# Hybrid recurrent/MoE decoder block: routing order, 8 KB weight runs, the order of the last expert pair and final norm, and the engines of the recurrence split

## The chip, the core and the metric

The kernel runs on one core of one Trainium2 chip. The metric is device time in microseconds (us) for one call; the changed kernel and the kernel before are timed in the same way. The core's engines are named as in the profile: PE (TensorE, matmuls), PEld (its weight loads), DVE (VectorE), ACT (ScalarE), POOL (GpSimd) and SP (the queue that issues the loads). The data are float32 throughout.

## What is computed

One decoder block over 512 tokens and 16 meta tokens, width 1024. Two mixers run side by side on the normed input (HGRN2, a gated linear recurrence of four heads, and RG-LRU, a convolution with a gated scan), are merged by two gates and projected. A mixture of experts follows: every token takes one of 4 groups and in it 2 of 8 experts, so that 32 experts of 3 x 2 MB of weights (gate, up, down) are all read once, 201 MB in all. Cut to the lines that matter here:

```python
def mixer(hn, w_in, ...):
    proj = hn @ w_in
    q_pre, f_pre, i_pre, og_pre, lx, ly, ga, gb = jnp.split(proj, idx, axis=-1)
    o_a = hgrn2_branch(q_pre, f_pre, i_pre, og_pre, lb, hg_norm_g)
    o_b = rglru_branch(lx, ly, conv_w, conv_b, w_r, b_r, w_i, b_i, lam)   # ends: h * gelu(ly)
    return (sigmoid(ga) * (o_a @ w_up_a) + sigmoid(gb) * (o_b @ w_up_b)) @ w_out

h = h + mixer(rmsnorm(h, norm1_g), ...)
hf = rmsnorm(h, norm2_g)
# group_logits -> top-1 group; exp_logits inside it -> top-2 experts and their weights
y = (silu(xb @ w_gate[e]) * (xb @ w_up[e])) @ w_down[e]      # xb: the tokens of expert e
h = h + sum over the two experts of weight * y
return rmsnorm(h, final_g)[:, N_META:]
```

## The kernel before, in words

**Mixers.** All products of the first half are made float32-exact from two fp32r parts: `split` (line 86) writes the rounded high part of a tensor with one engine and the rest (low part, a subtraction) with another. Weights come from `raw` slots and are split into three `hl` slots by `hl_tile`, high part by ACT or DVE (L88, L90), low part by POOL (L91); the matmuls of `dense` (L205) use high and low of both sides. The RG-LRU (`lru`, L623) walks over pairs of blocks; `finish` (L696) makes the scan of a pair, multiplies it by the gelu branch (`ge`, L711) and splits the result into `obH` and `obL` (L712), eight times in all. `merge` (L805) then needs the weights of the gates first, and `obH`/`obL` only for the product with `w_up_b`. PE and DVE and ACT are ordered by a scheduler in this half.

**Routing.** From line 1074 on, PE and DVE run in the order in which the code is written (`manual_schedule`). For each tile t of 128 tokens: `last` (output projection), `early` (square sum, transposes to `hT`, L900), `logits` (L922), `choose` (L928, then a row of small DVE operations that ends in `SEL`), `slots0` (rank of each token in its experts, L942, and the one-hot matrix `OH0` of the first expert pair, L978) and `dispatch` (L1105: two matmuls of 512 columns with `OH0` gather the tokens of the first pair into `px`). `XG`, its transpose `XS` and the first gate product follow.

**Experts.** The loop at L1158 takes two experts at a time (16 pairs, 64 token slots each, on the two column halves of PE). Weights come in pieces of 1 MB (L760, on SP) into some twenty slots; a piece holds two of the eight (gate, up) or one of the four (down) 128-row slices of **both** experts, so that one partition of it is two runs of 4 KB, one of each expert. A slot is free again when its last matmul has read it, and SP issues the next piece into it. PE per pair: `pgt` (gate), `pw`, `put` (up), `combine` of the pair before (`pcb`, L1055), transposes, `py` (down).

**The end.** The last pair's down weights come in half pieces (512 columns, runs of 2 KB). After the last pair each of the four token tiles gets its residual add (L1226, DVE), square sum (L1227, ACT), scaling (L1229, ACT; power on POOL, L1230), and two halves of the output: columns 0 to 511 by ACT or POOL in turn (L1233, L1235), 512 to 1023 by DVE (L1236), then the store (L1237).

Of the kernel before, what the change touches and what calls it, by code (L numbers as in the profile page):

```python
# [38 lines left out]
def hybrid_block_kernel(ctx: ExitStack, tc: tile.TileContext, x, meta, norm1_g, w_in, hg_lb,  # L39
# [583 lines left out]
    def lru():  # L623
# [6 lines left out]
        for b0 in range(0, NB, 2):  # L630
# [65 lines left out]
            def finish(b0=b0, bs=bs, XC=XC, RR=RR, TH=TH, GE=GE):  # L696
# [7 lines left out]
                for i, b in enumerate(bs):  # L704
# [7 lines left out]
                    split(obH[b // 4][:, b % 4], obL[b // 4][:, b % 4], ge, DVE, POOL)  # L712
# [28 lines left out]

    EW = [(w[0].rearrange("e (p k) c -> p e k c", p=128), nk) for w, nk in ((w_gate, 8), (w_up, 8), (w_down, 4))]
    last_p = NE // 2 - 1
    CUTS = [[(k, k + 2, 0, 512) for k in range(0, 8, 2)]] * 2 + [[(k, k + 1, 0, 1024) for k in range(4)]]
    pieces, pieces0 = [], []
    for p_ in range(last_p + 1):
        for m in range(3):
            cuts = CUTS[m]
            if p_ == 0 and m == 0:
                cuts = cuts[:2]  # L750
                pieces0 = [(0, 0, k, k + 1, 0, 512) for k in range(4, 8)]
            if p_ == last_p and m == 2:
                cuts = [(k, k + 1, c, c + 512) for c in (0, 512) for k in range(4)]
# [3 lines left out]

    def fetch(t_, s, piece):
        m, p, k0, k1, c0, c1 = piece
        SP.dma_start(t_, EW[m][0][:, 2 * p:2 * p + 2, k0:k1, c0:c1])  # L760
        for k in range(k0, k1):
            at.setdefault((m, p), {})[k, c0 // 512] = (t_[:, :, k - k0], c0, s)

    def prefetch(n=len(pieces)):
        while n and nxt[0] < len(pieces) and free:
# [3 lines left out]
            t_, s = slot([128, 2, piece[3] - piece[2], piece[5] - piece[4]], F32, "wx")  # L769
            fetch(t_, s, piece)  # L770

    def weight(tab, e, k, c0):

        t_, b, _ = tab.get((k, c0 // 512)) or tab[k, 0]
        return t_[:, e, c0 - b:c0 - b + 512]

    def take(m, p):
        tab = at.pop((m, p))
        return tab, sorted({s for _, _, s in tab.values() if s})
# [322 lines left out]
    def dispatch(t):  # L1102

        for half in range(2):
            PE.matmul(px[half], OH0[:, t], tk(h32, t, 512 * half, 512 * half + 512), start=(t == 0), stop=(t == 3))  # L1105
# [22 lines left out]
    dispatch(0)  # L1128
    early(3)
    choose(2, pls[2])  # L1130
    slots0(1)
    dispatch(1)
    pls.append(logits(3, hts[3]))
    slots0(2)
    choose(3, pls[3])
    dispatch(2)
    slots0(3)
    dispatch(3)
# [10 lines left out]
    SW = []  # L1149

    def feed(m, p, f):
        tab, ss = take(m, p)
        r = f(tab)
        give(*ss)
# [3 lines left out]
    for p in range(last_p + 1):  # L1158
# [14 lines left out]
        if p == last_p:  # L1173
            combine(back, 0)
            gfb = ms("A", [128, D], F32, "gfb")
            for half in range(2):
# [4 lines left out]
                ACT.activation(gfb[:, 512 * half:512 * half + 512], p_.rearrange("t a b -> t (a b)"), AF.Copy)  # L1181
        pu = feed(1, p, lambda w2: up_proj(w2, "put"))
# [135 lines left out]
```

## Time and profile before

| | us |
|---|---|
| median of 3 runs | 990.17 (989.74 to 991.3) |
| profiled execution, its own time | 990.63 |
| its span | 988.9 |
| PE busy | 917.6 (93%) |
| DVE / ACT / POOL busy | 453.1 / 255.9 / 247.8 |
| product lines: mixers `pj` L205 (hnH and hnL) | 251.8 and 149.1 |
| expert products `put`, `pgt`, `py` | 119.1, 115.7, 114.7 |

The span is cut into 40 slices on the page. PE reads 7 to 9 tenths in every slice, but matmuls are pipelined and their ends are modelled, so that this alone doesn't tell what bounds a stage. The transfer row tells it: 44 to 263 GB/s until slice 18, then 410, 334, 276, 373, and 408 to 410 in every slice up to the 38th. The granted clock of PE is 0.983 in the mean.

### The profile page before, as it was taken

Reading aid. Unit: us, or ns where it says so; the run is one execution under the profiler, and the core shown is the slowest. Engines: PE = TensorE matmul, PEld = TensorE weight load, DVE = VectorE, ACT = ScalarE, POOL = GpSimd, SP = SyncE. Lnnn points to the kernel's source line nnn. Section 1 sums busy time; section 2 is a strip of 40 time slices with the busy share of each in tenths; the row PEclk is TensorE's granted clock in tenths of the full one; section 3 lists DMA queues with packets and bytes.
Section 4 is the critical chain, followed back from the end, with each engine's and each line's share of the span. In section 5 each row is a group of like instructions: output and inputs, shape, how many; then the busy total and the mean of one; then the engine's idle time right before and its main releaser. Section 6 shows DMA issues by size and latency. Waiting matters only on the chain. (4 is left out here: it accounts for less than half of the span.)

```text
span 988.9 us, 12070 instructions
## 1 busy us (share of the span) xinstructions
PE 917.6 (93%) x4756; PEld 590.2 (60%) x4756; DVE 453.1 (46%) x924; ACT 255.9 (26%) x455; POOL 247.8 (25%) x167
## 2 busy tenths in 40 slices
PE   7989999989988999999978999999998988889893
PEld 5979998979967888888733444444442433323341
DVE  5668458786784323323552443343431433224323
ACT  6445535966760000000310111000010100011013
POOL 3542442344456454555100000000000000000004
PEclk9989999999999999999999999999999999999997
DMA  6222112112472322239979999999999999999982
GB/s 217 66 73 77 44 54 86 54 55 86 159 263 85 99 92 92 79 128 410 334 276 373 408 408 408 408 408 408 408 409 408 410 408 409 408 408 409 409 346 88
DMA packets 94151, 251.45 MB, mean 254 GB/s; under 512 B 6507, under 2 KB 39359, under 8 KB 94090
## 3 DMA queue, kind: packets, MB, share of 16 engines
q1 hardware_dynamic: 91352, 244.61, 64.7%
q0 software_dynamic: 2160, 3.91, 1.1%
q10 hardware_dynamic: 578, 2.10, 0.5%
q8 instruction: 39, 0.64, 0.3%
q14 instruction: 22, 0.18, 0.0%
HBM read 250.37 MB, written 4.19 MB: 257 GB/s over the span
## 5 line engine op out<-in xcount | busy, mean ns | idle before, releaser
L205 PE MATMUL pj<-hnH,hl 128*128 128x512 f32 (+1 forms) x960 | 251.8, 352 | 10.5 <-POOL hl L91 8.2
L91 POOL TENSOR_TENSOR hl<-raw,hl 128x1024 fp32r<-128x1024 f32 (+1 forms) x76 | 174.7, 2301 | 196.1 <-ACT hl L88 99.6
L205 PEld LDWEIGHTS pj<-hnH,hl 128*128 128x128 f32 x960 | 163.0, 191 | 34.4 <-POOL hl L91 9.5
L205 PE MATMUL pj<-hnL,hl 128*128 128x512 f32 (+1 forms) x480 | 149.1, 348 | 0.0
L1022 PE MATMUL put<-wx,XS 128*64 128x512 f32 x512 | 119.1, 606 | 18.6 <-DMA wx<-in_w_up_dram 18.5
L1022 PE MATMUL pgt<-wx,XS 128*64 128x512 f32 x512 | 115.7, 601 | 3.0 <-DMA wx<-in_w_gate_dram 2.7
L1041 PE MATMUL py<-wx,HG 128*64 128x512 f32 x512 | 114.7, 596 | 2.4 <-DMA wx<-in_w_down_dram 1.7
L995 POOL DMA_INDIRECT XG<-HD,idx x15 | 15.1, 1008 | 400.2 <-DVE OHT L1002 382.5
L205 PEld LDWEIGHTS pj<-hnL,hl 128*128 128x128 f32 x480 | 85.0, 191 | 10.1
L1022 PEld LDWEIGHTS put<-wx,XS 128*64 128x64 f32 x512 | 34.0, 137 | 89.6 <-issue 53.8
L1022 PEld LDWEIGHTS pgt<-wx,XS 128*64 128x64 f32 x512 | 36.5, 138 | 78.4 <-issue 69.5
L1058 DVE TENSOR_TENSOR h<-h,pcb 128x512 f32<-128x512 f32 x124 | 75.5, 679 | 7.4 <-PE pcb L1055 7.4
L1041 PEld LDWEIGHTS py<-wx,HG 128*64 128x64 f32 x512 | 34.8, 137 | 69.7 <-issue 60.6
L1028 DVE SCALAR_TENSOR_TENSOR HG<-put,sw,HG 128x512 f32<-128x512 f32 x16 | 12.0, 752 | 120.6 <-PE put L1022 114.8
L1049 DVE SCALAR_TENSOR_TENSOR Y<-py,sw,Y 128x512 fp32r<-128x512 f32 x31 | 23.3, 751 | 89.9 <-ACT Y L1048 89.9
L90 DVE CAST hl<-raw 128x1024 fp32r<-128x1024 f32 (+1 forms) x40 | 35.7, 892 | 58.4 <-PE pj L205 58.4
L1055 PE MATMUL pcb<-Y,OHT 128*128 128x512 f32 x248 | 62.0, 401 | 0.0
L1036 ACT ACTIVATE HG<-pht 128x512 f32<-128x512 f32 x16 | 9.6, 598 | 195.1 <-PE pht L1035 195.1
L1055 PEld LDWEIGHTS pcb<-Y,OHT 128*128 128x128 f32 x248 | 45.2, 188 | 23.8 <-issue 14.6
L1048 ACT ACTIVATE Y<-py,sw 128x512 fp32r<-128x512 f32 x31 | 21.3, 687 | 105.3 <-PE py L1041 101.4
L205 PE MATMUL pj<-obH,hl 128*128 128x512 f32 x128 | 40.6, 393 | 0.0
L88 ACT ACTIVATE hl<-raw 128x1024 fp32r<-128x1024 f32 (+1 forms) x36 | 36.1, 1004 | 5.8 <-PE pj L312 3.1
(266 smaller groups left out, 1086.7 us busy)
## 6 DMA issues: line engine op xcount, KB each, us to landing
wx<-in_w_up_dram SPq DMA_DIRECT2D x64, 1024.0 KB, 18.6
wx<-in_w_gate_dram SPq DMA_DIRECT2D x62, 1024.0 KB, 19.0
wx<-in_w_down_dram SPq DMA_DIRECT2D x60, 1024.0 KB, 19.0
raw<-in_w_in_dram SPq DMA_DIRECT2D x24, 1024.0 KB
raw<-in_w_up_b_dram SPq DMA_DIRECT2D x4, 1024.0 KB
raw<-in_w_out_dram SPq DMA_DIRECT2D x4, 1024.0 KB, 4.9
wx<-in_w_down_dram SPq DMA_DIRECT2D x8, 512.0 KB, 17.1
h<-in_x_dram SPq DMA_DIRECT2D x2, 1024.0 KB
```

What stands on the lines that cost most here:

```text
L88: ACT.activation(hi, src, AF.Copy)
L90: he.tensor_copy(hi, src)
L91: le.tensor_sub(lo, src, hi.bitcast(F32))
L205: PE.matmul(o[:, :c1 - c0], w[:, k, :], hsl(a, k, c0, c1), start=(k == 0 and w is wh and a is aH), stop=(k == nk - 1 and w is wl))
L995: POOL.indirect_dma_start(XG, None, HD[:], bass.IndirectOffsetOnAxis(ap=idx, axis=0), bounds_check=T - 1, oob_is_err=False)
L1022: PE.matmul(p_[CAP * e:CAP * e + CAP], XS[:, k, CAP * e:CAP * e + CAP], weight(w2, e, k, 0), start=(k == 0), stop=(k == 7))
L1028: DVE.scalar_tensor_tensor(HG, pu, sw[:, 2:3], HG, op0=OP.mult, op1=OP.mult)
L1041: PE.matmul(p_[CAP * e:CAP * e + CAP], HT[:, 128 * k + CAP * e:128 * k + CAP * e + CAP], weight(w2, e, k, 512 * half), start=(k == 0), sto ...
L1048: ACT.activation(yh, p_, AF.Copy, scale=sw[:, 0:1])
L1049: DVE.scalar_tensor_tensor(Y[half][:, 1], p_, sw[:, 0:1], yh.bitcast(F32), op0=OP.mult, op1=OP.subtract)
L1055: PE.matmul(p_, oht[:, 128 * t:128 * t + 128], Y[half][:, i], start=(i == 0), stop=(i == 1))
L1058: DVE.tensor_add(hs, hs, p_)
```

## The change

Four edits in one. (1) In `finish`, `obH` is written by ACT in place of DVE, and `obL` by DVE in place of POOL. (2) In the routing, `early(3)` stands ahead of the first `dispatch`, `slots0(1)` ahead of `choose(2)`, `logits(3)` ahead of most of the dispatches, and `dispatch` is cut into its two matmuls so that they can stand between other steps. (3) A weight piece is still 1 MB, but of **one** expert: four slices of gate or up, or two of down, so that one partition is one run of 8 KB. Pieces of the two experts take turns. The first gate's second half (`pieces0`) and the last pair's down pieces keep their 2 KB runs. (4) The final gain `gfb` is spread over the partitions in the 15th pair instead of the 16th, into a weight slot kept back for it; in the 16th pair both halves of `combine` stand ahead of the up product; the final norm is cut into two loops, the copies of columns 0 to 511 go to ACT for three tiles and to DVE for the last, and POOL has none.

```diff
-                    split(obH[b // 4][:, b % 4], obL[b // 4][:, b % 4], ge, DVE, POOL)
+                    split(obH[b // 4][:, b % 4], obL[b // 4][:, b % 4], ge, ACT, DVE)
...
-    CUTS = [[(k, k + 2, 0, 512) for k in range(0, 8, 2)]] * 2 + [[(k, k + 1, 0, 1024) for k in range(4)]]
+    CUTS = [[(e, e + 1, k, k + 4, 0, 512) for k in (0, 4) for e in (0, 1)]] * 2 + \
+        [[(e, e + 1, k, k + 2, 0, 1024) for k in (0, 2) for e in (0, 1)]]
...
-                pieces0 = [(0, 0, k, k + 1, 0, 512) for k in range(4, 8)]
+                pieces0 = [(0, 0, 0, 2, k, k + 1, 0, 512) for k in range(4, 8)]
             if p_ == last_p and m == 2:
-                cuts = [(k, k + 1, c, c + 512) for c in (0, 512) for k in range(4)]
+                cuts = [(0, 2, k, k + 1, c, c + 512) for c in (0, 512) for k in range(4)]
...
+    def note(tab, t_, s, cut):
+        e0, e1, k0, k1, c0, c1 = cut
+        for e in range(e0, e1):
+            for k in range(k0, k1):
+                for c in range(c0, c1, 512):
+                    tab[e, k, c] = (t_[:, e - e0, k - k0, c - c0:c - c0 + 512], s)
+
     def fetch(t_, s, piece):
-        m, p, k0, k1, c0, c1 = piece
-        SP.dma_start(t_, EW[m][0][:, 2 * p:2 * p + 2, k0:k1, c0:c1])
...
+        m, p, e0, e1, k0, k1, c0, c1 = piece
+        SP.dma_start(t_, EW[m][0][:, 2 * p + e0:2 * p + e1, k0:k1, c0:c1])
+        note(at.setdefault((m, p), {}), t_, s, piece[2:])
...
-    dispatch(0)
     early(3)
+    dispatch(0, 0)
+    slots0(1)
     choose(2, pls[2])
-    slots0(1)
-    dispatch(1)
     pls.append(logits(3, hts[3]))
+    dispatch(0, 1)
+    dispatch(1, 0)
     slots0(2)
     choose(3, pls[3])
-    dispatch(2)
+    dispatch(1, 1)
+    for half in range(2):
+        dispatch(2, half)
     slots0(3)
-    dispatch(3)
+    for half in range(2):
+        dispatch(3, half)
...
+        if (m, p) == (2, last_p - 2):
+            gfb_s.append(ss.pop())
...
-        if p == last_p:
-            combine(back, 0)
-            gfb = ms("A", [128, D], F32, "gfb")
+        if p == last_p - 1:
+            gfb = big_or_late(gfb_s[0], [128, D], F32, "gfb")
...
+        if p == last_p:
+            for half in range(2):
+                combine(back, half)
         pu = feed(1, p, lambda w2: up_proj(w2, "put"))
         glu(pg, pu, sw)
-        if p:
-            for half in range(p == last_p, 2):
+        if 0 < p < last_p:
+            for half in range(2):
                 combine(back, half)
...
         POOL.tensor_tensor(rs, rs, mhalf[:, :1], op=OP.pow)
-        o = outs[t][0]
-        if t % 2:
+    for t in range(4):
+        o, hs, rs = outs[t][0], tk(h32, t, 512), SS[:, 2, t:t + 1]
+        if t < 3:
             ACT.activation(o[:, :512], u0[:, t], AF.Copy, scale=rs)
-        else:
-            POOL.tensor_scalar(o[:, :512], u0[:, t], rs, None, op0=OP.mult)
         DVE.scalar_tensor_tensor(o[:, 512:], hs, rs, gfb[:, 512:], op0=OP.mult, op1=OP.mult)
+        if t == 3:
+            DVE.tensor_scalar(o[:, :512], u0[:, t], rs, None, op0=OP.mult)
         SP.dma_start(out2[128 * t:128 * t + 128], o)
```

The instructions that move, as they stand on their engines. On DVE, where the last pair of RG-LRU blocks is finished and the gates' weights are split (`ge` is the finished branch, `hl` a weight's two parts, `gA` the gate); a minus is before, a plus is now:

```order
 L711 SCALAR_TENSOR_TENSOR ge_2512<-ge_2512,th_2511 128x512 x2
-L90 CAST obH_2674<-ge_2512 128x512 x2
+L864 MEMSET rw_3899 128x8x4
 L90 CAST hl_2903<-raw_2852 128x1024
-L856 MEMSET rw_3899 128x8x4
-L857 MEMSET rw_3899 128x8x24
-L817 TENSOR_TENSOR gA_2831<-gA_2831,pj 128x512
+L91 TENSOR_TENSOR obL_2675<-ge_2512,obH_2674 128x512 x2
```

The weight's high part now stands directly behind the finished branch, and the subtraction for `obL` behind it. On POOL at the same place:

```order
 L91 TENSOR_TENSOR hl_2880<-raw_2760,hl_2880 128x512
-L91 TENSOR_TENSOR obL_2675<-ge_2512,obH_2674 128x512 x2
 L91 TENSOR_TENSOR hl_2903<-raw_2852,hl_2903 128x1024
 L91 TENSOR_TENSOR hl_2922<-raw_2852,hl_2922 128x1024
```

Two subtractions are gone from between the weights' low parts. On PE in the routing, from the logits of the third tile on, before (`plg` logits, `px` dispatch, `pT` transposes of the last tile, `prk` ranks):

```order
L922 MATMUL plg<-hT_4145,rw_3899 64x128 x8
L1105 MATMUL px_4194<-h_2827,OH_194_4136 128x512
L1105 MATMUL px_4195<-h_2827,OH_194_4136 128x512
L900 MATMUL pT<-ident,h_2829 128x128 x8
L928 MATMUL plg<-rt_3919 128x40
L942 LDWEIGHTS onesb
L942 MATMUL prk<-SEL,onesb 128x32
L942 LDWEIGHTS tri
L942 MATMUL prk<-SEL,tri 128x32
L1105 MATMUL px_4194<-h_2827,OH_194_4136 128x512
L1105 MATMUL px_4195<-h_2827,OH_194_4136 128x512
L922 MATMUL plg<-hT_4203,rw_3899 64x128 x8
```

The same place now:

```order
L930 MATMUL plg<-hT_4145,rw_3899 64x128 x8
L908 MATMUL pT<-ident,h_2829 128x128 x8
L1112 MATMUL px_4194<-h_2827,OH_194_4136 128x512
L950 LDWEIGHTS onesb
L950 MATMUL prk<-SEL,onesb 128x32
L950 LDWEIGHTS tri
L950 MATMUL prk<-SEL,tri 128x32
L936 MATMUL plg<-rt_3919 128x40
L930 MATMUL plg<-hT_4201,rw_3899 64x128 x8
L1112 MATMUL px_4195<-h_2827,OH_194_4136 128x512
L1112 MATMUL px_4194<-h_2827,OH_194_4136 128x512
```

The last tile's transposes moved ahead of the first dispatch, and its logits (second `plg<-hT`) ahead of the second tile's dispatch. On DVE in the final norm, before:

```order
L1226 TENSOR_TENSOR h_2827<-h_2827,pcb 128x512
L1236 SCALAR_TENSOR_TENSOR o_6644<-h_2827,ssf,gfb_6588 128x512
L1226 TENSOR_TENSOR h_2827<-h_2827,pcb 128x512
L1236 SCALAR_TENSOR_TENSOR o_6645<-h_2827,ssf,gfb_6588 128x512
L1226 TENSOR_TENSOR h_2829<-h_2829,pcb 128x512
```

and now, all four tiles:

```order
L1241 TENSOR_TENSOR h_2827<-h_2827,pcb 128x512 x2
L1241 TENSOR_TENSOR h_2829<-h_2829,pcb 128x512 x2
L1250 SCALAR_TENSOR_TENSOR o_6644<-h_2827,ssf,gfb_6455 128x512
L1250 SCALAR_TENSOR_TENSOR o_6645<-h_2827,ssf,gfb_6455 128x512
L1250 SCALAR_TENSOR_TENSOR o_6646<-h_2829,ssf,gfb_6455 128x512
L1250 SCALAR_TENSOR_TENSOR o_6647<-h_2829,ssf,gfb_6455 128x512
L1252 TENSOR_SCALAR o_6647<-u_387_6642,ssf 128x512
```

The residual adds no longer stand behind the scaled outputs of the tile before.

## Rows read from the trace of the kernel before

**Rows 1.** Stretches: length, busy us (count) per engine, clock, DMA share, GB/s
```profile
480.00:535.00 55.00, 46.15 (x269) 23.61 (x267) 25.38 (x100) 13.42 (x24) 3.57 (x6) 1.00 0.84 312
535.00:940.00 405.00, 382.64 (x1809) 158.13 (x1809) 143.20 (x313) 37.22 (x56) 13.85 (x14) 0.99 1.03 409
```

**Rows 2.** Timeline, mixers' end: start, us, what [idle before <- releaser]
```profile
292.99 0.76 DVE L90 CAST obH<-ge 128x512 fp32r<-128x512 f32 x2
293.49 3.67 POOL L91 TENSOR_TENSOR obL<-ge,obH 128x512 fp32r<-128x512 f32 x2 [5.83 <-DVE obH L90]
293.66 0.69 DVE L90 CAST hl<-raw 128x1024 fp32r<-128x1024 f32 x1
...
297.12 7.54 POOL L91 TENSOR_TENSOR hl<-raw,hl 128x1024 fp32r<-128x1024 f32 x3
...
299.51 0.73 PE L205 MATMUL pj<-hnH,hl 128*128 128x512 f32 x2 [4.31 <-POOL hl L91]
```

**Rows 3.** Timeline, routing: PE, and the DVE row that begins choose(2)
```profile
490.46 1.98 PE L1105 MATMUL px<-h,OH 128*128 128x512 f32 x4
493.59 0.26 DVE L929 SCALAR_TENSOR_TENSOR rt<-plg,RS,brow 128x40 f32<-128x40 f32 x1 [1.23 <-PE prk L942]
...
496.25 1.98 PE L1105 MATMUL px<-h,OH 128*128 128x512 f32 x4 [2.73 <-DVE OH L978]
498.16 1.10 PE L922 MATMUL plg<-hT,rw 128*64 128x128 f32 x16
...
503.19 1.98 PE L1105 MATMUL px<-h,OH 128*128 128x512 f32 x4 [0.61 <-DVE OH L978]
...
507.52 7.09 PE L1022 MATMUL pgt<-wx,XS 128*64 128x512 f32 x32 [0.34 <-DVE XS L1015]
```

**Rows 4.** SP timeline (issues) and the stretch around it, columns as in Rows 1
```profile
530.59 2.08 SPq L760 DMA_DIRECT2D wx<-in_w_up_dram  x3
...
530.00:535.00 5.00, 3.14 (x17) 0.86 (x13) 1.69 (x3) 1.11 (x2) 0.00 (x0) 1.00 0.91 321
```

**Rows 5.** Queues: packets, MB, share of 16 engines; windows 560:940 (two), 332.9:336.6, 976:977, 983.2:983.7
```profile
q1 hardware_dynamic: 39329, 151.62, 99.9%
q8 instruction: 13, 0.21, 0.2%
...
q1 hardware_dynamic: 1040, 1.05, 85.9%
...
q1 hardware_dynamic: 101, 0.36, 88.1%
...
q14 instruction: 1, 0.01, 3.9%
```

**Rows 6.** Timeline of PE, last pair: gate's end, gfb, up, down
```profile
942.56 1.94 PE L1022 MATMUL pgt<-wx,XS 128*64 128x512 f32 x8 [0.53 <-DMA wx<-in_w_gate_dram]
...
946.46 2.05 PE L1180 MATMUL pgf<-gf,ident 8*128 8x128 f32 x16
...
948.44 7.09 PE L1022 MATMUL put<-wx,XS 128*64 128x512 f32 x32
...
958.80 5.37 PE L1041 MATMUL py<-wx,HG 128*64 128x512 f32 x24 [0.75 <-ACT HG L1036]
```

**Rows 7.** Timeline, final norm: first and last tile
```profile
970.10 0.69 DVE L1226 TENSOR_TENSOR h<-h,pcb 128x512 f32<-128x512 f32 x1 [1.22 <-PE pcb L1225]
...
978.83 2.12 POOL L1235 TENSOR_SCALAR o<-u,ssf 128x512 f32<-128x512 f32 x1
...
980.14 0.63 ACT L1227 ACTIVATE sqf<-h 128x512 f32<-128x512 f32 x1 [2.04 <-DVE h L1226]
...
980.90 0.29 ACT L1229 ACTIVATE ssf<-ssf 128x1 f32<-128x1 f32 x1
981.27 0.57 POOL L1230 TENSOR_TENSOR ssf<-ssf,mhalf 128x1 f32<-128x1 f32 x1 [0.33 <-ACT ssf L1229]
981.88 0.72 ACT L1233 ACTIVATE o<-u,ssf 128x512 f32<-128x512 f32 x1 [0.69 <-POOL ssf L1230]
```

More of the change, by code (lines that the diff above doesn't have):

```diff
@@ L768, in prefetch @@
             nxt[0] += 1
-            t_, s = slot([128, 2, piece[3] - piece[2], piece[5] - piece[4]], F32, "wx")
+            e0, e1, k0, k1, c0, c1 = piece[2:]
+            t_, s = slot([128, e1 - e0, k1 - k0, c1 - c0], F32, "wx")
             fetch(t_, s, piece)
     def weight(tab, e, k, c0):
-        t_, b, _ = tab.get((k, c0 // 512)) or tab[k, 0]
-        return t_[:, e, c0 - b:c0 - b + 512]
+        return tab[e, k, c0][0]
     def take(m, p):
         tab = at.pop((m, p))
-        return tab, sorted({s for _, _, s in tab.values() if s})
+        return tab, sorted({s for _, s in tab.values() if s})
     def gate(dst):
@@ L1100, in slots0, with dispatch @@
         onehots(OH0, RK[:, :, 0:2], [t])
-    def dispatch(t):
-        for half in range(2):
-            PE.matmul(px[half], OH0[:, t], tk(h32, t, 512 * half, 512 * half + 512), start=(t == 0), stop=(t == 3))
+    def dispatch(t, half):
+        PE.matmul(px[half], OH0[:, t], tk(h32, t, 512 * half, 512 * half + 512), start=(t == 0), stop=(t == 3))
     for t in range(2):
@@ L1148, in hybrid_block_kernel @@
     onehots(OH, RK[:, :, 0:2])
-    SW = []
+    SW, gfb_s = [], []
     def feed(m, p, f):
@@ L1230, in hybrid_block_kernel @@
         POOL.tensor_tensor(rs, rs, mhalf[:, :1], op=OP.pow)
-        o = outs[t][0]
-        if t % 2:
+    for t in range(4):
+        o, hs, rs = outs[t][0], tk(h32, t, 512), SS[:, 2, t:t + 1]
+        if t < 3:
             ACT.activation(o[:, :512], u0[:, t], AF.Copy, scale=rs)
-        else:
-            POOL.tensor_scalar(o[:, :512], u0[:, t], rs, None, op0=OP.mult)
         DVE.scalar_tensor_tensor(o[:, 512:], hs, rs, gfb[:, 512:], op0=OP.mult, op1=OP.mult)
+        if t == 3:
+            DVE.tensor_scalar(o[:, :512], u0[:, t], rs, None, op0=OP.mult)
         SP.dma_start(out2[128 * t:128 * t + 128], o)
-    give(*ss_, s, s2, *[s for _, s in outs])
+    give(*ss_, s, s2, *gfb_s, *[s for _, s in outs])
     order.__exit__(None, None, None)
@@ L1256, in hybrid_block_kernel @@
                         tabs.append({})
-                        for k0, k1, _, c1 in cuts:
-                            t_, s = slot([128, 2, k1 - k0, c1], F32, "wx")
-                            SP.dma_start(t_, w[:, bass.ds(i4 * 4 + 2 * i, 2), k0:k1, :])
+                        for cut in cuts:
+                            e0, e1, k0, k1, _, c1 = cut
+                            t_, s = slot([128, e1 - e0, k1 - k0, c1], F32, "wx")
+                            SP.dma_start(t_, w[:, bass.ds(i4 * 4 + 2 * i + e0, e1 - e0), k0:k1, :])
                             ss.append(s)
-                            for k in range(k0, k1):
-                                tabs[-1][k, 0] = (t_[:, :, k - k0], 0, s)
+                            note(tabs[-1], t_, s, cut)
                     glu(up_proj(tabs[0], "pgt"), up_proj(tabs[1], "put"), sw)
```

2 lines of the change are left out of this document (removed).

## The prediction, made before the changed kernel ran

> **What bounds the kernel now.** I read the stretches first, then inside each stretch the wait that ends last. Up to some 490 us PE works through the mixers with few gaps, so a gap there is worth its whole length. Between 480 and 535 the transfers run at 312 GB/s, and from 535 to 940 at 409 GB/s with the DMA engines' share at 1.03 [rows 1]: the queue of weight loads alone fills 99.9% of the sixteen engines there [rows 5]. In that stretch the weights are the limit, and PE waits for them, as the 0.53 us ahead of the last gate product shows [rows 6]. So the time is made of three parts: the moment from which the stream is never again without a free slot; the stream from there to the last pair's gate weights; and what PE, DVE and ACT do after those have landed. The last moment at which the stream lacks slots is at 530.6: SP issues three up pieces at once, when the first pair's down product gives their slots back, and the transfers around it run at 321 GB/s [rows 4]; after 535 the mean is 409.
>
> **Part 1, the recurrence split.** The last stall of PE in the mixers ends at 299.51, after 4.31 us, with a weight's low part from POOL [rows 2]. POOL began that at 297.12 (three in 7.54, 2.5 each), because the two `obL` subtractions stood before it from 293.49 on for 3.67; the high part it needs was cast by DVE at 293.66 in 0.69 [rows 2]. In the changed order DVE casts that weight in the place of the `obH` casts (292.99), so it ends near 293.8 and POOL, with nothing before it, at 296.4. PE goes on at some 296.5: **-3.0**. An earlier stall of the same kind, behind the pair of blocks before, shrinks too, but then PE only waits longer here. Bounds: ACT gets two copies more ahead of DVE's chain; at the 0.72 of a copy of this size [rows 7] they would take 1.4 back (-1.6). The other end is the whole 3.67. DVE's later subtractions lie beside PE's products, which need `obL` only in a later product; if that cover were gone they would cost some 0.7 each, as an add of this size does [rows 7]. Behind 300 PE has no gap up to the routing, so the 3.0 goes through.
>
> **Part 2, the routing.** PE does the first dispatch (490.46, 1.98), waits 2.73 for a one-hot that DVE makes only after choose(2) (begun 493.59), dispatches the second tile at 496.25, and only then, at 498.16, makes the last tile's logits, on which choose(3), the ranks and the last dispatch (503.19) hang; the first gate product starts at 507.52 [rows 3]. In the new order the last tile's transposes take 490.5 to 491.6 (as long as the logits' 1.10), the half dispatch (1.98/2) ends at 492.6 and the ranks at 492.8, so DVE has the one-hot at 493.3 and choose(2) (2.2 long by the same rows: 493.59 to the one-hot's 496.25, less 0.5 for that) ends at 495.5. The logits run at 493.1, when ACT has copied the transposes (two copies of about 0.7 from 491.6 on), in place of 498.16; choose(3) on DVE runs from 497.1 to 499.3. PE meanwhile has five half dispatches, the ranks and the small product of choose(3), to 499.8, then the ranks and the one-hot of the last tile, and the last dispatch starts at 500.95 in place of 503.19: **-2.2**. So PE, no longer DVE, is late there, and the bounds are -1.4 (each cross-engine step 0.1 dearer than I took) and -2.7, the whole wait. `weights()` and `by_slot` follow on DVE and PE as before and move with it. SP's order doesn't change; the four small loads of the first gate wait for the tile that the last logits read, so they are issued some 5 us earlier and land about when needed.
>
> **Part 3, the pieces.** Same 1 MB, same places, but the two slots that a product reads first are now free after four slices instead of one after two. For the issue at 530.6 this is one slice of the down product later, 7.09/8: **+0.8** (0 to +1.8, the latter for a piece of an up product). The moment from which the stream is never without work thus moves by -3.0 - 2.2 + 0.8 = -4.4.
>
> From there to the last gate (531 to 942, 411 us) the price is the packet. From the queue rows [rows 5]: 151.62 MB in 4 KB packets took 99.9% of 16 x 380 us, 164.1 ns each; the 1 KB loads of the mixers 85.9% of 16 x 3.7 us for 1.05 MB, 49.6 ns each. A line through both gives 38.2 ns per KB and 11.4 ns per packet, so 316.8 ns for 8 KB against 328.2 for two of 4 KB: 3.5% less. No weight load of 8 KB is in the trace; one packet of that size is, an instruction fetch: 3.9% of 16 x 0.5 us, 312 ns, where a 4 KB packet of the output store, with free engines too, takes 88.1% of 16 us for 0.36 MB, 160 ns: 2.7% less than two. I take 3.0%: **-12.3** (-11.1 to -14.4 by these rows). A far row speaks against it: instruction packets of 16 KB took 0.2% of 16 x 380 us for 13, some 0.94 us each, 57 ns per KB where 4 KB packets cost 40. They go to another memory, so I price them as a rival only.
>
> First the row, then the rule: the fit has a fixed part of 9 to 11 ns per packet. The Trainium skill (page "DMA: Bandwidth & Descriptors", section "Why small descriptors are slow (HBM only)") gives a fixed overhead of about 3 cycles per packet, for beats of 32 bytes. By that page, as an estimate, 8 KB would cost 259 cycles for 262, 1.1% less, and the sum would have -4.5 in place of -12.3. The trace's 1 KB packets, at 49.6 ns, are dearer than a quarter of 164.1 by 8.6 ns, more than the rule allows; so I keep the rows, and the rule's size is a rival.
>
> **Part 4, the end.** After the last gate piece PE takes 16.2 us to the first down product (942.56 to 958.80), with `gfb` (2.05) in it [rows 6]. Now `gfb` lies in the 15th pair, where PE waits for weights anyway (without that cover 2.05 would come back), but four slices of the gate (3.55) are left when the last piece lands instead of two (1.94), and both halves of combine precede the up product (7.09), 2.0 each by what lies between the gate's end at 944.5 and 946.46. From up's end (955.5) to the first down product lie 3.3, with one half of combine in them; without it the chain of DVE, PE and ACT through the hidden layer is between 1.3 and 3.3, and I take 2.4, since three engines follow each other there: 3.55 + 4.0 + 7.1 + 2.4 = 17.05, **+0.8** (-0.3 to +1.7). In the final norm a tile's chain runs from add to output, and DVE's next add stands behind it: 970.10 for the first, 982.6 the last end [rows 7]. Now the adds go ahead and ACT is the late engine: square 0.76 with its read-out, scaling 0.29, copy 0.72, 1.75 per tile, in the order square, copy of the tile before, scaling. First power ready at 972.5, first copy to 973.2, third to 976.7, last scaling and power to 977.7, then DVE's 0.75 and about 0.55: 979.0 instead of 982.6, **-3.6** (-2.5 with 0.3 more per tile; -4.2 with ACT's overlaps). POOL's copies of 2.12 are gone. The stores stand 1.7 apart, more than the 1.3 that half a MB takes at 400 GB/s, so none queues.
>
> **Sum.** -4.4 - 12.3 + 0.8 - 3.6 = -19.5. Against the profiled execution's own time (990.63, that is its span of 988.9 and 1.7 around it) this is 971.1; that execution lies 0.46 above the median of the runs, less than the sum is sure to. Forecast **971.1**, by its own bounds 967 to 976.
>
> **Rivals.**
> (a) The packets don't grow: 8 KB runs are carried as two packets of 4 KB, or the memory side and not the packet sets 409 GB/s. For it: the rate is the same to 1 GB/s over 400 us. Against it: 1 KB packets, too, cost what a per-packet price says. Then -12.3 falls away: 983.4.
> (b) The packet's fixed part is a third of the fit's, 3.8 ns of 328.2 saved, 1.2%: -4.8 in place of -12.3, 978.6. For it: the 1 KB rows are one short burst, whose packets may be slower for other reasons. The Trainium skill's page above would have it so.
> (c) The early gains don't arrive: the stream's last lack of slots comes from the coarser pieces, or PE loses Part 1 to DVE, whose subtractions run beside POOL. Then -4.4 becomes 0: 975.5.
> (d) Slower: an 8 KB packet costs more than two of 4 KB, at the memory's port or in the queue between other packets. Without Part 3's gain the rest is -7.2, so it decides from 1.8% on, a packet over 334 ns. A third of the way to the 16 KB packets' price per KB, 14% more, would cost 57: 1041; at 5% more, 345 ns, the time is 1004.
>
> **How the numbers follow.** Forecast 0.64; (a) 0.12, (b) 0.12, (c) 0.08, (d) 0.04. The range 966 to 982 holds the forecast's own, (b) and (c), and leaves out (a), (d) and a little below. A measurement of this kernel can tell some 0.2%, 2 us, from no change: faster 0.95 (all but (d) and a piece of (a)), same 0.02, slower 0.03.
>
> **What would show it.** In the profile after: 418 to 424 GB/s in the stretch that showed 409, with about half the packets; the POOL release near 299.5 some 3 us earlier; the first gate product near 502.3; the last gate wait near 926; from there to the first down product 17 us; the four adds of the final norm in a row and a last output some 9 us after the first. A rate of 409 kills Part 3; a late product that waits for POOL still, Part 1; a last dispatch that waits for DVE over 1 us, Part 2; ACT idle between the tiles of the norm, Part 4.

## The result and the profile after

The changed kernel takes **965.88 us** (median of four runs, 964.29 to 968.70), the kernel before in the same comparison 990.46 (four runs, 989.74 to 991.30). The ratio is **0.9755, 95% interval 0.9730 to 0.9779**. The forecast was 971.1 with a range of 966 to 982: the sign is right, the gain is 5 us larger than forecast, and the median lies 0.12 us below the range. The profiled execution of after took 965.6 us, with a span of 963.8.

I read the changed kernel in the order of the prediction's steps. First the mixers' end, as in [rows 2]: the timeline of after (start us, us, engine and instruction, idle time before it and its releaser).

```profile
287.99 0.66 DVE L90 CAST hl<-raw 128x1024 fp32r<-128x1024 f32 x1
288.56 3.43 DVE L91 TENSOR_TENSOR obL<-ge,obH 128x512 fp32r<-128x512 f32 x2
...
288.72 2.72 POOL L91 TENSOR_TENSOR hl<-raw,hl 128x1024 fp32r<-128x1024 f32 x1 [6.10 <-DVE hl L90]
...
291.50 0.73 PE L205 MATMUL pj<-hnH,hl 128*128 128x512 f32 x2 [2.01 <-POOL hl L91]
```

As forecast, DVE casts the weight in the place of the `obH` casts, and POOL follows at once. But PE goes on at 291.50, where it went on at 299.51: 8.0 us earlier, not 3.0.

Next the routing, as in [rows 3] and [rows 4]: the last output projection, the last dispatch, the first gate product (PE), and the three up pieces that SP issues together.

```profile
478.15 1.64 PE L1097 MATMUL po<-hl,mg 128*128 128x512 f32 x6
...
489.89 1.98 PE L1112 MATMUL px<-h,OH 128*128 128x512 f32 x4 [0.62 <-DVE OH L986]
...
494.21 7.09 PE L1030 MATMUL pgt<-wx,XS 128*64 128x512 f32 x32 [0.34 <-DVE XS L1023]
...
518.13 2.04 SPq L769 DMA_DIRECT2D wx<-in_w_up_dram  x3
```

The first gate product has moved by 13.3 us (507.52 to 494.21), the issue by 12.5 (530.59 to 518.13). Then the stream: the stretches of after (length, busy us of PE, PEld, DVE, ACT and POOL, granted clock, DMA share, GB/s), and the weight queue in the window 560 to 900 (packets, MB, share of sixteen engines), where the kernel before has the second queue row.

```profile
480.00:535.00 55.00, 49.36 (x250) 20.22 (x252) 23.10 (x95) 9.04 (x14) 3.05 (x4) 0.97 0.88 338
530.00:920.00 390.00, 380.86 (x1798) 171.09 (x1794) 141.71 (x305) 38.47 (x58) 13.86 (x14) 1.00 1.01 420
...
q1 hardware_dynamic: 19125, 139.26, 98.7%
```

```profile
q1 hardware_dynamic: 35153, 135.52, 99.8%
```

420 GB/s in place of 409, with 54% of the packets. Last the end of the program, as in [rows 6] and [rows 7]: PE in the last pair, then DVE in the final norm (first add, last add, last output).

```profile
920.64 3.65 PE L1030 MATMUL pgt<-wx,XS 128*64 128x512 f32 x14 [0.40 <-DMA wx<-in_w_gate_dram]
...
937.63 5.37 PE L1049 MATMUL py<-wx,HG 128*64 128x512 f32 x24 [0.75 <-ACT HG L1044]
...
948.93 0.69 DVE L1241 TENSOR_TENSOR h<-h,pcb 128x512 f32<-128x512 f32 x1 [1.22 <-PE pcb L1240]
...
951.50 0.69 DVE L1241 TENSOR_TENSOR h<-h,pcb 128x512 f32<-128x512 f32 x1 [0.17 <-PE pcb L1240]
...
957.10 0.48 DVE L1252 TENSOR_SCALAR o<-u,ssf 128x512 f32<-128x512 f32 x1
```

From these rows the 25.1 us between the two spans can be laid out as a chain of distances between the same events. Two rows of before stand in no group so far: PE's release near 203, from a wait for the state update of the recurrence, and the last output projection.

```profile
203.64 0.51 PE L205 MATMUL pj<-hnH,hl 128*128 128x512 f32 x1 [2.27 <-DVE st L556]
...
487.71 1.64 PE L1089 MATMUL po<-hl,mg 128*128 128x512 f32 x6
```

The release stands at 202.48 after; the next section says why that much is no effect of an edit.

| From | to | before | after | difference | forecast |
|---|---|---|---|---|---|
| start | PE's release near 203 | 203.64 | 202.48 | -1.2 | 0 |
| that | last output projection | 284.07 | 275.67 | -8.4 | -3.0 |
| that | last dispatch | 15.48 | 11.74 | -3.7 | -2.2 |
| that | last wait for a gate piece ends | 439.37 | 430.75 | -8.6 | -11.5 |
| that | first down product of the last pair | 16.24 | 16.99 | +0.8 | +0.8 |
| that | first add of the norm | 11.30 | 11.30 | 0 | 0 |
| that | last output's end | 12.53 | 8.65 | -3.9 | -3.6 |

So the two terms of the end are right, the routing gave more than forecast, the stream less, and the mixers far more. These misses have both signs and partly cancel: the first three rows together gave 8.1 us more than forecast, the stream took 2.9 back. The experiments ask why.

### The profile page after: what moved, and what is told of

It reads as the page before. It is cut to its first block, busy times and chain, and to the rows that moved or that the text cites. A ratio compares the mean times of both kernels' runs of the same rounds, so it can differ in the third digit from the quotient of the medians.

```text
span 963.8 us, 12064 instructions
## 1 busy us (share of the span) xinstructions
PE 918.1 (95%) x4756; PEld 601.8 (62%) x4756; DVE 451.9 (47%) x925; ACT 260.6 (27%) x464; POOL 231.9 (24%) x157
## 4 chain that ended last, share of the span: by engine, by line
## 5 line engine op out<-in xcount | busy, mean ns | idle before, releaser
L1030 PE MATMUL pgt<-wx,XS 128*64 128x512 f32 x512 | 119.7, 601 | 2.4 <-DMA wx<-in_w_gate_dram 2.0
L1030 PEld LDWEIGHTS pgt<-wx,XS 128*64 128x64 f32 x512 | 41.1, 138 | 76.7 <-issue 67.8
L1030 PEld LDWEIGHTS put<-wx,XS 128*64 128x64 f32 x512 | 38.3, 138 | 76.8 <-issue 58.3
L1049 PEld LDWEIGHTS py<-wx,HG 128*64 128x64 f32 x512 | 39.6, 137 | 62.7 <-issue 58.0
L1063 PEld LDWEIGHTS pcb<-Y,OHT 128*128 128x128 f32 x248 | 45.3, 188 | 22.4 <-issue 13.1
L90 DVE CAST hl<-raw 128x1024 fp32r<-128x1024 f32 (+1 forms) x40 | 32.9, 823 | 54.6 <-PE pj L205 54.6
L1035 ACT ACTIVATE HG<-pgt,sw 128x512 f32<-128x512 f32 x16 | 11.0, 688 | 103.5 <-PE pgt L1030 103.5
```

The costliest lines, as they stand in the source:

```text
L90: he.tensor_copy(hi, src)
L1030: PE.matmul(p_[CAP * e:CAP * e + CAP], XS[:, k, CAP * e:CAP * e + CAP], weight(w2, e, k, 0), start=(k == 0), stop=(k == 7))
L1035: ACT.activation(HG, pg, AF.Silu, scale=sw[:, 2:3])
L1049: PE.matmul(p_[CAP * e:CAP * e + CAP], HT[:, 128 * k + CAP * e:128 * k + CAP * e + CAP], weight(w2, e, k, 512 * half), start=(k == 0), sto ...
L1063: PE.matmul(p_, oht[:, 128 * t:128 * t + 128], Y[half][:, i], start=(i == 0), stop=(i == 1))
```

## The experiments

**Each edit alone.** Four kernels are the kernel before with one of the edits. Their diffs are the corresponding parts of the change shown above; the first is one line:

```
-  split(obH[b // 4][:, b % 4], obL[b // 4][:, b % 4], ge, DVE, POOL)
+  split(obH[b // 4][:, b % 4], obL[b // 4][:, b % 4], ge, ACT, DVE)
```

> The kernel before with one edit alone: the recurrence outputs' high parts copied by ScalarE, their low parts subtracted by VectorE (the split of obH and obL). Forecast's theory (only GpSimd's queue ahead of the last stalled weight gets shorter): the time falls by 3.0 us, PE's release by GpSimd's low part moves from 299.5 to 296.5, the last dispatch from 503.2 to 500.2. Theory from the trace after (the stall goes at two places and the clock doesn't drop behind it): -9.6 us, the release near 291.5, the last output projection near 478.2 in place of 487.7. Rival (a part of that shift lies ahead of the first recurrence output and is no effect of any edit): -8.2 us, and PE at 190 us where it was before.

> The kernel before with one edit alone: the routing's steps in the other order (dispatch in halves, last tile's logits earlier). Forecast's theory: -2.2 us, from the last output projection to the first gate product 17.6 us in place of 19.8. Theory from the trace after: -3.75 us, 16.06 us between the two. Rival (the weights' stream doesn't follow PE there): the distance shrinks and the time stays within 1 us of before.

> The kernel before with one edit alone: expert weights in pieces of one expert and 8 KB runs. Forecast's theory: -12.3 for the packets, +0.8 for the slot that is freed later, +1.6 for four gate slices left behind the last piece: -9.9 us, the stream at 421 GB/s. Theory from the trace after (2.5 to 2.8% off the packets): -7.8 to -8.6 us, 419 to 420 GB/s. Rival (the stream's gain belongs to the other edits): 409 GB/s and +2.4 us.

> The kernel before with one edit alone: the spread gate row made a pair earlier, both halves of combine ahead of the last up product, and the final norm's loop in two (adds first, copies by ScalarE and VectorE). Forecast's theory: -3.6 for the norm and -0.8 for the last pair (without the coarser pieces two slices are left, not four): -4.4 us. Theory from the trace after: -4.7 us, 8.65 us from the first add to the last end in place of 12.5. Rival (one slot fewer in the last two pairs costs the stream something): -2 to -3 us, with PE waiting for weights longer at the last gate.

| Edit alone | median us (before: 990.07) | ratio, 95% interval | worth in us | in the profile |
|---|---|---|---|---|
| recurrence split | 982.51 | 0.9919 (0.9905 to 0.9933) | -8.0 | -6.7 |
| routing order | 986.00 | 0.9957 (0.9943 to 0.9971) | -4.3 | -2.6 |
| pieces with 8 KB runs | 982.52 | 0.9926 (0.9912 to 0.9940) | -7.3 | -8.2 |
| last pair and norm | 985.18 | 0.9955 (0.9941 to 0.9969) | -4.5 | -4.9 |

The worth is one less the ratio, times 990; each has some 1.4 us either way. The last column is what the distance from PE's release near 203 to the last output's end changed in the profiled execution, from 779.0 in the kernel before. The four worths add up to -24.1, and the whole change gives -24.3. In the profiles they add up to -22.4, and after has -23.9, of which 1.6 come from the clock, as shown below. Within these errors the edits don't depend on one another. The split is worth -8.0 with an interval of -6.6 to -9.4, so the forecast's -3.0 falls, and the rival of that run holds: part of the -9.6 seen in after's trace is no effect of an edit. The release near 203 stands at 203.64, 201.90, 202.32 and 201.99 in four kernels whose code up to there is the same (before, and the routing, the pieces and the end alone); what differs is the granted clock between 40 and 80 us, 0.91 in the first and 0.96 in the other three. The edit of the end gave the 15.3 us from the last gate wait to the first down product (940.87 to 956.14) that its forecast wanted (15.45); no cost of the held slot can be seen.

The pieces alone fall short of their -9.9, which lies outside the interval of -5.9 to -8.7. In their profile the way from the last dispatch to the last gate wait is 429.39 us (before 439.37), -10.0 where -11.5 was forecast, and the four slices left behind the last piece cost 1.7 (17.96 to the first down product) where +1.6 was.

The routing alone, PE's timeline: the last output projection, two groups of half dispatches, the last dispatch.

```profile
486.01 1.64 PE L1089 MATMUL po<-hl,mg 128*128 128x512 f32 x6
...
492.09 1.98 PE L1104 MATMUL px<-h,OH 128*128 128x512 f32 x4
493.91 0.20 PE L942 MATMUL prk<-SEL,onesb 128*128 128x32 bf16 x2
...
494.21 2.82 PE L1104 MATMUL px<-h,OH 128*128 128x512 f32 x6
...
497.74 1.98 PE L1104 MATMUL px<-h,OH 128*128 128x512 f32 x4 [0.62 <-DVE OH L978]
```

From the first to the last of these rows 11.73 us pass, in after 11.74, before 15.48 (487.71 to the 503.19 of [rows 3]). PE has no gap in this stretch but the 0.62, and a group that is listed with 1.98 is followed after 1.82. Not all of this gets through: from the last dispatch to the last gate wait the kernel takes 440.51 us, 1.1 more than before. The weight queue moves 0.5 MB more in that time (from the issue of the three up pieces on, 164.45 MB in place of 163.98), which is 1.1 us at 409 GB/s. So by the profile 2.6 us reach the end; by the times it is 2.9 to 5.6.

**What of the split matters.** Two more kernels are the kernel before with half of that edit each:

```
s_dve:      split(..., ge, DVE, DVE)
s_actpool:  split(..., ge, ACT, POOL)
```

> The kernel before with the recurrence outputs split by VectorE alone (copy and subtraction), GpSimd and ScalarE out of it. Theory A (GpSimd's queue ahead of the stalled weights is the cause): PE's way from the wait near 203 to the last output projection falls from 284.1 us to 277 to 278, as with the split by ScalarE and VectorE (277.5), the time by 6 to 8 us. Theory B (what counts is the copy that VectorE no longer makes ahead of a weight's cast): the way stays at 283 to 284.1 and the time within 1.5 us of before.

> The kernel before with the copies of the recurrence outputs by ScalarE and the subtractions by GpSimd as before. Theory A (GpSimd's queue): the two stalls behind GpSimd's low parts stay at 2.9 and 4.3 us, the way from 203 to the last output projection at 283.5 to 285 us, the time within 1.5 us of before. Theory B (VectorE's copy): the way falls to near 278, the time by 6 us or more.

The first took 988.79 us beside 989.54 (ratio 0.9992, 0.9982 to 1.0002), the second 986.04 (0.9963, 0.9949 to 0.9977). Theory A falls, since GpSimd's queue empty by itself brings nothing; theory B doesn't hold either, since the copies alone bring 3.7 of 8.0. The traces tell why. The way is taken here from the begin of the wait near 203, since that wait changes, to the last output projection. The last columns cut it in three: to DVE's finish of the last pair of blocks (L711), from there to PE's release behind the stall near 295, and on to the projection.

| | copy, subtraction by | wait near 203 | stall near 275 | stall near 295 | way | to the finish | to the release | to the projection |
|---|---|---|---|---|---|---|---|---|
| before | DVE, POOL | 2.27 | 2.93 | 4.31 | 286.3 | 90.4 | 7.7 | 188.2 |
| s_dve | DVE, DVE | 5.57 | 1.69 | 1.10 + 1.63 | 285.6 | 91.1 | 6.2 | 188.2 |
| s_actpool | ACT, POOL | 1.93 | none | 3.09 | 282.7 | 87.7 | 5.8 | 189.2 |
| e_split | ACT, DVE | 2.53 | 0.27 | 2.00 | 280.0 | 87.1 | 4.7 | 188.2 |
| after | ACT, DVE | 2.54 | 0.27 | 2.01 | 278.2 | 86.8 | 4.7 | 186.7 |

First the stall near 275, which the prediction knew but held to be worth nothing. Timeline of POOL and PE in the kernel before:

```profile
272.34 3.12 POOL L91 TENSOR_TENSOR obL<-ge,obH 128x512 fp32r<-128x512 f32 x2 [5.78 <-DVE obH L90]
275.43 2.80 POOL L91 TENSOR_TENSOR hl<-raw,hl 128x1024 fp32r<-128x1024 f32 x1
...
278.28 0.74 PE L205 MATMUL pj<-hnH,hl 128*128 128x512 f32 x2 [2.93 <-POOL hl L91]
```

And of POOL in s_actpool:

```profile
270.26 2.42 POOL L91 TENSOR_TENSOR hl<-raw,hl 128x1024 fp32r<-128x1024 f32 x1 [6.64 <-DVE hl L90]
272.63 3.48 POOL L91 TENSOR_TENSOR obL<-ge,obH 128x512 fp32r<-128x512 f32 x2
```

With the copy on ACT, DVE casts the weight while ACT copies, so the weight's low part reaches POOL ahead of `obL`, and the stall is gone although POOL does as much as before. It comes back near 295 only, where `obL` still gets in between (3.09). Moving the subtractions away from POOL takes that one down to 2.00.

What is the stall near 275 worth by itself? The kernel with the routing alone (e_routing) answers, whose code up to there is that of before: in its profile the granted clock fell behind this stall, in that of before it did not. The two stalls of PE in e_routing, then the stretch behind the first (length, PE busy, granted clock, DMA share, GB/s) in before and in e_routing:

```profile
276.57 0.73 PE L205 MATMUL pj<-hnH,hl 128*128 128x512 f32 x2 [2.96 <-POOL hl L91]
...
297.79 0.74 PE L205 MATMUL pj<-hnH,hl 128*128 128x512 f32 x2 [2.84 <-POOL hl L91]
```

```profile
276.00:284.00 8.00, 5.72 (x25) 1.00 0.31 110
```

```profile
276.00:284.00 8.00, 7.43 (x25) 0.79 0.42 139
```

PE lost 1.5 us to the clock, and its second stall is 1.5 shorter (2.84 for 4.31); the second release comes 21.2 us behind the first in both. So time that PE wins or loses between the two stalls doesn't move the second release: the chain on DVE, ACT and POOL that ends in it waits for PE nowhere between them. The prediction was right that PE would only wait longer.

What moves the release is that chain. Its last finish on DVE, before and then in e_split:

```profile
291.80 1.27 DVE L711 SCALAR_TENSOR_TENSOR ge<-ge,th 128x512 f32<-128x512 f32 x2
```

```profile
287.73 1.27 DVE L711 SCALAR_TENSOR_TENSOR ge<-ge,th 128x512 f32<-128x512 f32 x2
```

Counted from the wait near 203 the finish is 3.4 us earlier, and from the finish to PE's release 7.7 us become 4.7. The 3.4 are gathered along the way, and two of the places can be named, where DVE stood behind or beside a subtraction of POOL. One is the scaling in the recurrence's norm, which waits for a power that POOL makes behind two subtractions for `obL`, before and in e_split:

```profile
240.17 0.69 DVE L577 TENSOR_TENSOR on<-po,rs 128x512 f32<-128x512 f32 x1 [3.40 <-POOL rs L107]
```

```profile
237.25 0.69 DVE L577 TENSOR_TENSOR on<-po,rs 128x512 f32<-128x512 f32 x1 [1.75 <-POOL rs L107]
```

The other is the cast of a weight in the stall near 275, which took 2.83 us beside POOL's subtraction of 275.43 and takes 0.68 in e_split, while its neighbour takes 1.1 more there. No run takes the places apart.

Then what s_dve loses near 203, its timeline of DVE, POOL and PE there:

```profile
201.09 3.23 POOL L91 TENSOR_TENSOR hl<-raw,hl 128x1024 fp32r<-128x1024 f32 x1 [3.44 <-ACT hl L88]
...
202.11 2.76 DVE L91 TENSOR_TENSOR obL<-ge,obH 128x512 fp32r<-128x512 f32 x1
204.79 0.68 DVE L711 SCALAR_TENSOR_TENSOR ge<-ge,th 128x512 f32<-128x512 f32 x1
205.40 0.33 DVE L556 SCALAR_TENSOR_TENSOR st<-st,gend,pS 128x128 f32<-128x128 f32 x1
...
205.79 0.79 PE L205 MATMUL pj<-hnH,hl 128*128 128x512 f32 x1 [5.57 <-DVE st L556]
```

The subtraction, whose median in after is 0.68 us, takes 2.76 beside a subtraction of POOL and ends 0.55 behind it. The state update that PE waits for stands behind it, 3 us late. The Trainium skill ("SBUF — State Buffer", section "Who interferes with whom") says that a VectorE instruction with two inputs in SBUF contends with a GpSimd instruction that reads SBUF, and calls the ports that they share an exclusive lock; this trace agrees, with 2.76 for 0.68. In e_split the subtraction at this place falls ahead of POOL's and takes 0.68. So the edit's gain is a matter of places in two queues, and needs both halves. In s_actpool 1.0 us of its gain is lost again behind its last stall, where the clock is low for longer (0.76 between 292 and 306, 0.88 in before).

**The clock behind the stall.** e_split and after have the same two stalls, yet the way differs by 1.8 us, 1.6 of them behind the last stall. Stretches behind the last stall, PE alone (length, busy, granted clock, DMA share, GB/s), of before, after and e_split in turn:

```profile
297.00:304.00 7.00, 4.49 (x13) 0.76 0.08 17
```

```profile
297.00:304.00 7.00, 7.00 (x32) 1.00 0.57 161
```

```profile
291.00:297.00 6.00, 4.53 (x13) 0.72 0.10 25
```

Before and in e_split the granted clock is at the lower of its two levels (1.2 of 2.4 GHz) for part of the stretch behind PE's last stall; in after it stays at the full one. 6 us at 0.72 are 1.7 us of full clock lost, about the difference of the two ways behind the stall. Eight kernels of this study have the new split: from the release near 203 to the last output projection three take 275.7 to 276.0 us (after, p_2k, n_copies), and five 277.5; between 288 and 302 the mean clock is 1.00 in the three and 0.88 in all of the five. The four kernels with the old split and no other edit there take 284.1 each. So the split is worth 6.6 us, and another 1.6 to 1.8 when the clock doesn't drop; what decides that, no run here shows.

**The packet's size.** Two kernels are after with the pieces and slots as they are, each piece of one expert fetched by two or four transfers along its slices (`d` slices in each; for the 2 KB runs the down slices are cut in halves of their columns too, not shown):

```
-  SP.dma_start(t_, EW[m][0][:, 2 * p + e0:2 * p + e1, k0:k1, c0:c1])
+  for k in range(k0, k1, d):
+      SP.dma_start(t_[:, :, k - k0:k - k0 + d], EW[m][0][:, 2 * p + e0:2 * p + e1, k:k + d, c0:c1])
```

> The kernel after, pieces and slots as they are, but each piece of one expert fetched by two transfers of half a MB whose runs are 4 KB. Packet theory: back to 408 to 409 GB/s, the stream 10 to 11 us longer, 976 to 977 us. Rival (the rate comes from the pieces of one expert or their order): 419 to 420 GB/s and 966 us. Rival (twice the transfers cost SP's queue something by themselves): under 405 GB/s.

> The kernel after, but each piece of one expert fetched by four transfers of a quarter of a MB whose runs are 2 KB. By the line through 1 KB and 4 KB packets (38.2 ns per KB and 11.4 ns per packet): 87.8 ns for a packet of 2 KB, 382 GB/s, the stream of 399 us 40 us longer, 1006 us. By a fixed part of a third (3.8 ns): 164.1/2 + 1.9 = 84 ns, some 400 GB/s, 20 us longer, 986 us. By the rival that packets don't matter: 966 us.

With 4 KB runs 975.59 us (ratio to before 0.9852, 0.9834 to 0.9871), with 2 KB runs 999.63 (1.0112, 1.0083 to 1.0141). The weight queue in the window 560 to 900, first p_4k, then p_2k:

```profile
q1 hardware_dynamic: 37224, 135.54, 99.9%
```

```profile
q1 hardware_dynamic: 70048, 127.55, 101.9%
```

4 KB: 408 GB/s as before, so neither the shape nor the order of the pieces carries the rate, and rival (a) is out. The queue's rows, MB over packet size and share of 16 x 340 us, give 316 ns for a packet of 8 KB, 164 for 4 KB and 89 for 2 KB: a step from 4 to 8 KB saves 12 ns, one from 4 to 2 KB costs 14. The line through 1 KB and 4 KB packets had said 316.8, 164.1 and 87.8; its fixed part of 11.4 nearly holds at both ends, and rival (b), with a third of it, is out. Twice as many transfers cost nothing that shows: p_4k has the 164 ns of before. The 2 KB kernel stands 34 us above after where 40 was forecast, with a rate of 385 GB/s where 382 was.

**The final norm.** Two kernels are after with one half of its norm each: n_order keeps the adds ahead but gives two tiles' copies back to GpSimd, n_copies keeps GpSimd free but makes a tile's output before the next tile's add.

```
n_order:
-  if t < 3:
+  if t % 2:
       ACT.activation(o[:, :512], u0[:, t], AF.Copy, scale=rs)
+  else:
+      POOL.tensor_scalar(o[:, :512], u0[:, t], rs, None, op0=OP.mult)
-  if t == 3:
-      DVE.tensor_scalar(o[:, :512], u0[:, t], rs, None, op0=OP.mult)
n_copies:
-  for t in range(4):
-      o, hs, rs = outs[t][0], tk(h32, t, 512), SS[:, 2, t:t + 1]
+      o = outs[t][0]
```

> The kernel after, the four adds of the final norm ahead as they are, but GpSimd scaling the first halves of two tiles as before (2.12 us each). Theory (the order carries the gain, the late engine is ScalarE): the first add to the last end takes 8.7 to 10 us. Rival (GpSimd's two copies behind its four powers are late then): 10 to 12.5 us, so that neither the order nor the copies alone carry the 3.9 us.

> The kernel after, without GpSimd's copies in the final norm as it is, but each tile's outputs made before the next tile's add, as before. Theory (the order carries the gain): 11 to 12.5 us from the first add to the last end. Rival (GpSimd's copies were the cost): 9 to 10 us.

There is one time of each, so the distance in the trace is compared; it is 8.65 or 8.66 in all six kernels with the new norm and 12.52 to 12.54 in four with the old one. From the first add to the last end n_order takes 9.75 us (950.53 to 960.28), n_copies 12.89 (949.56 to 962.45); before it was 12.53 and after it is 8.65. The order alone gives 2.8, the copies alone nothing (0.4 lost), both 3.9: a free GpSimd pays only behind the new order. The end of n_order, POOL and DVE:

```profile
956.85 2.12 POOL L1251 TENSOR_SCALAR o<-u,ssf 128x512 f32<-128x512 f32 x1
958.94 0.56 POOL L1245 TENSOR_TENSOR ssf<-ssf,mhalf 128x1 f32<-128x1 f32 x1
...
959.53 0.75 DVE L1252 SCALAR_TENSOR_TENSOR o<-h,ssf,gfb 128x512 f32<-128x512 f32 x1 [2.00 <-POOL ssf L1245]
```

The last tile's power stands behind a copy of 2.12 us on POOL.

**A better last pair?** In after four gate slices are left when the last gate piece lands, and PE waits 0.95 and 0.75 us for the hidden layer. Two kernels change this: v_end cuts the last two gate pieces into two slices of both experts and puts the second half of the combine into those two gaps; v_end2 cuts the up pieces of that pair in the same way.

```
+  if p_ == last_p and m == 0:        (v_end2: m < 2)
+      cuts = cuts[:2] + [(0, 2, k, k + 2, 0, 512) for k in (4, 6)]
...
   if p == last_p:
-      for half in range(2):
-          combine(back, half)
+      combine(back, 0)
...
+  if p == last_p:
+      combine(back, 1, range(2))
   hidden_T()
+  if p == last_p:
+      combine(back, 1, range(2, 4))
```

> The kernel after with two changes in the last pair: the last two gate pieces hold two slices of both experts (4 KB runs), so that two slices are left when the last one lands; and the second half of the last combine stands in two halves in the gaps in which PE waits for the hidden layer (0.95 and 0.75 us). From the terms of the last pair: -1.7 for the slices, -1.8 for the combine, +0.15 for 2 MB in smaller packets: 962.5 us, 13.6 us from the last gate wait to the first down product in place of 17.0. Rival (the last pair is bound by the weights' stream by then): PE waits for up or down weights instead, and the time stays within 1 us of 966.

> The kernel with the finer last gate pieces and the combine in the gaps, and the last pair's up weights cut in the same finer way. Theory (in the kernel after, PE's chain and the stream reach the last up weights at the same moment, so only finer up pieces let the 3.5 us through): two slices of up are left behind the last landing in place of four, so from the three up pieces issued at the start of the full stream to the first down product 417.7 us in place of 419.5, and 964.2 us. Rival (the down weights, in 2 KB runs, are late then): PE waits for down weights, 419 us or more, and 966 us.

v_end took 966.03 us (ratio 0.9745, 0.9732 to 0.9759), v_end2 965.28 (0.9745, 0.9725 to 0.9765): neither can be told from after (0.9755). In v_end the rival holds. PE in its last pair:

```profile
933.82 3.65 PE L1032 MATMUL put<-wx,XS 128*64 128x512 f32 x14 [0.62 <-DMA wx<-in_w_up_dram]
```

The wait for the gate is gone, and one for an up piece with four slices left has come. From the issue of the three up pieces to the first down product v_end takes 419.46 us (520.53 to 939.99), after 419.50. In v_end2 that wait is gone too:

```profile
519.88 2.04 SPq L771 DMA_DIRECT2D wx<-in_w_up_dram  x3
...
937.27 5.37 PE L1051 MATMUL py<-wx,HG 128*64 128x512 f32 x24
```

417.39 us, 2.1 less than after and as expected (417.7). The theory holds by the trace. The times don't show the 2.1, which is no more than the half width of their interval, and the profiled execution lost 1.6 to the clock near 295.

## Why the prediction was right, and where it was too small

**What bounds the kernel** was right: the mixers' gaps on PE, the moment from which the stream always has slots, the stream, and the chain behind the last gate. Each edit moved the time by about what it moved in its stretch, the routing's by less.

**Part 1 failed in size: -3.0 forecast, -8.0 measured alone (-6.7 in the profile), bounds -1.6 to -3.7.** What it priced was right: DVE casts the weight in the copies' place, POOL follows, and from DVE's last finish to PE's release 7.7 us became 4.7, the -3.0 of the forecast. It was also right that the earlier stall of PE is worth nothing by itself. The step that failed is the start of that sum: the place of the `obH` casts, 292.99, was taken as fixed, so the chain on DVE and ACT ahead of it was put at nothing. Some of its instructions, too, stood beside or behind POOL's subtractions, and it ends 3.4 us earlier. 3.4 and 3.0 make the 6.3 by which the way of e_split is shorter than that of before (286.3 and 280.0, with rounding). After has 1.8 more, 1.6 of it from the clock, a term that the prediction didn't have.

**Part 2 was right in mechanism, too small at the last dispatch: -2.2 forecast, -3.7 by the distance, of which 2.6 reach the end in the profile; -4.3 by the time alone.** PE, not DVE, is late there, as forecast. Most of the miss is that the chain was made of listed durations, which overlap: the row of 1.98 is followed after 1.82. A last dispatch forecast at 500.95, in the time of before, stands at 499.4 (497.74, and 1.70 for that run's earlier last output projection). My bound of -2.7, "the whole wait", was no bound: behind that wait DVE's later steps moved too.

**Part 3.** The slot that comes free later: +0.8 forecast, +0.84 measured (last dispatch to the issue 27.40 before, 28.24 after). The packet's price was right: 316.8 ns forecast, 316 measured. The term was too large all the same: -12.3 forecast, -10.8 for the pieces alone (from the issue to the last gate wait 411.97 before, 401.15 then), -9.8 between p_4k and after (last dispatch to last gate wait 440.51 and 430.75). The rate rose by 2.7%, not by the packet's 3.5: the queue's share fell from 99.8 to 98.7%, so a part of what each packet saves comes back as time between packets. 2.7% of the 402 us from that issue to the last gate wait is 10.9, as in the pieces alone; why p_4k and after lie 1.1 closer, no run shows. With the +0.8 and the 1.1 that the routing's order costs the stream, the pieces' -10.8 comes to -8.9, near the -8.6 of the table. The Trainium skill ("DMA: Bandwidth & Descriptors", section "Why small descriptors are slow (HBM only)") has a fixed overhead of about 3 cycles per packet, by which, as an estimate, 8 KB packets would take 1.1% less. Here the rate rose by 2.7%, and from 4 to 2 KB the packets' time per byte rose by 8%.

**Part 4** was right: +0.75 for +0.8, -3.9 for -3.6. ACT is the late engine of the norm, as forecast, and the order carries most of it.

**The rivals**: (a) and (b) are excluded by p_4k and p_2k, (d) by 420 GB/s, and (c), that the early gains don't arrive, by the two edits alone: the split's gain reached the end in full, and of the routing's 3.7 us all but 1.1. The median lies at the very edge of the range because Part 1's bounds came from the last stall only; that it lies no further out is luck, since the stream's miss of 2.9 us went the other way.

## What to carry to other kernels

When an engine stalls on a chain of other engines, price the chain and not the stall: an earlier stall of the waiting engine can be worth nothing, while every instruction that the edit speeds up along the chain counts, also far ahead of the stall. The clock that drops behind a stall may come back as well. A hand-over between two engines may be helped in full only when both queues ahead of it get shorter (here 0.1% and 0.4% for the halves, 0.8% for both), so cost each half of such an edit apart. For a long weight stream, longer runs are worth a fixed price per packet that could be read beforehand from two packet sizes in the trace, less a part for the queue's own idle time; coarser pieces give some of it back where a product waits for the last one.

## What the runs showed of the hardware that I had not expected

- Behind the same stall of 2.0 us the granted clock dropped in five kernels' profiled executions (mean 0.88 between 288 and 302, some 1.6 us lost) and stayed at 1.00 in three.
- A DVE subtraction of 0.68 us took 2.76 beside one of POOL, and two of them 3.43 in after (288.56), where they cost nothing since PE waits for POOL there.
- PE is nearly the bound of the stream now. PE's waits between 535 and 918 us (total, times, longest), before and then after:

```profile
PE put L1022 <- DMA wx<-in_w_up_dram: 16.6, 21, 2.3
PE pgt L1022 <- DMA wx<-in_w_gate_dram: 2.1, 4, 0.5
...
PE py L1041 <- DMA wx<-in_w_down_dram: 1.4, 4, 0.5
```

```profile
PE put L1030 <- DMA wx<-in_w_up_dram: 7.1, 5, 3.0
PE pgt L1030 <- DMA wx<-in_w_gate_dram: 1.6, 4, 0.6
```

20.1 us of waiting for weights have become 8.7. An estimate from this: of a further gain in the stream's rate about that much can reach the end, which no run here tried.
